# A tenth Strassen pair in three gate units, stage loads on SyncE, and other places for the Strassen steps

## Chip, cores and metric

One core of one Trainium2 chip. The metric is device microseconds of one execution; the program is run several times and the median is taken.

## What is computed

A decoder block over 256 tokens with 4096 channels, in fp32 (cut to the lines that cost time):

```python
h = rmsnorm(x, norm_w)                                       # 256 x 4096
u_p, z_p, u_c, b_c, c_c, z_c, g_logit = split(h @ w_in)      # w_in: 4096 x 20480
y_pool = causal_multiscale_pool(u_p, pool_w, pool_scale) * silu(z_p)
y_conv = causal_gated_shortconv(u_c, b_c, c_c, conv_w, conv_b) * silu(z_c)
br     = einsum('bsnc,ncd->bsnd', stack(y_pool, y_conv), w_branch)   # 2 x (2048 x 4096)
merged = sum_n sigmoid(g_logit + gate_b) * br
out    = rmsnorm(x + merged @ w_out, final_norm_w)           # w_out: 4096 x 4096
```

## The kernel before, in words

**Units and steps.** Every product is cut into units of 1024 output columns: 20 units on x (names cu, cc, cz, cb, pz, pu and the eight gate units g0_0 to g1_3, in the order g0_0, g1_0, g0_1, g1_1, g0_2, g1_2, g0_3, g1_3), 8 branch units (b0_0 to b1_3) and 4 output units (o0 to o3). A unit is a row of steps, 16 in the x and output units and 8 in the branch units. One step multiplies a pair of 128-channel blocks of the operand, kept in SBUF in `arena`, with 256 x 1024 weights that SyncE loads into one of three buffers `raw`. Two units carry the pooling as extra steps.

**Three products for one.** Each operand is held as a high part and the rest in fp32r, so that one product is three matmuls: high x high, high x rest, rest x high. For the weights ScalarE (ACT) writes the high part into `ring` and VectorE (DVE) the rest, by a subtraction (L72 is the one line that records all of DVE's tensor-tensor operations, L69 all of ACT's, L87, L91 and L94 the DMAs of SyncE and GpSimd; L1301 records the matmuls).

**P steps and Strassen steps.** A P step takes 2 token halves x 2 column halves x 2 blocks x 3 = 24 matmuls of 128x512. An S step does the 2x2 block product with 7 sums in place of 8 products (Winograd's form of Strassen): 21 matmuls. For it DVE must form weight sums: `V` (two sums, 128x1024), then `W` (two steps of 128x512), and split three of the raw blocks, V and W into `ring`. In a *helped* S step DMA forms V's sums: SyncE loads one block twice into a half of the tile E or R, GpSimd adds the other blocks to it with an accumulating DMA (`move_add`, L94), and `raw` gets 768 KB instead of 1024 KB. An S step needs the operand's own Strassen sums too, so only some pairs have them: x has 7 pairs stored plain (0 to 6) and 9 with sums (7 to 15).

**What sets the order.** The tables `PLACES` (and `OUT` for the output units) say at which of a unit's 16 steps the S steps stand; a unit with nine places uses the nine pairs 7 to 15 for them, and the others as P steps. `HELPED` says which S steps of a unit may be helped; whether one is depends on E or R being free by then. The preparation of weights runs up to three steps ahead of the matmuls, as far as `ring` (62 blocks; a P step takes 16, an S step 28) has room.

**Operands of the next stage.** From the end of g0_3 the places in `arena` that come free are filled with the operands of the branch units. `pop_fill`, called every 6 matmuls, starts a load of 256 KB from DRAM (`Fill.fetch`, by GpSimd's queue, L91) into one of the stages `sa`, `sb` or, during g1_3, the two halves of Y, and 8 calls later puts the work on it in the program: for a Strassen pair four sums on DVE, then a split on ACT and on DVE. In the output units the operands come from `m_d` in the same way.

**Gate units.** After the last Strassen product of a gate unit DVE joins the shared sums into R, GpSimd adds the bias by `move_add` (R<-in_gate_b, 1 MB), 12 calls later DVE adds E to R, ACT takes the sigmoid and GpSimd stores R to `gates_d`.

Of the kernel before, what the change touches and what calls it, by code (L numbers as in the profile page):

```python
# [26 lines left out]
F32 = mybir.dt.float32  # L27
F32R = mybir.dt.float32r
# [4 lines left out]
P = 128  # L33
T = 256
# [8 lines left out]
NP_X, NS_X = 7, 9  # L43
# [13 lines left out]
def hybrid_block(ctx: ExitStack, tc: tile.TileContext, x, x_t, norm_t, w_first, w_in, pool_w, pool_scale,  # L57
# [10 lines left out]
    def act(dst, src, func=AF.Copy, **kw):  # L68
        return pin(nc.scalar.activation(dst, src, func, **kw))  # L69
# [16 lines left out]
    def load(dst, src):  # L86
        return pin(nc.sync.dma_start(dst, src))  # L87

    def move(dst, src):

        return pin(nc.gpsimd.dma_start(dst, src))  # L91
# [8 lines left out]
    dram = ctx.enter_context(tc.tile_pool(name="dram", bufs=1, space=bass.MemoryType.DRAM))  # L100
# [33 lines left out]
    lower, upper = {}, {}  # L134
# [54 lines left out]
    Q3, Q5, Q6, Q7, A12, A22, A11, A21 = range(8)  # L189

    class Operand:


        def __init__(self, kind, view, region):
            self.kind, self.view, self.region = kind, view, region
            self.ready = False

        def block(self, part, i):

            return self.view[:, part, i]  # L200
# [373 lines left out]
    x_ops = make_ops(NP_X, NS_X, [("p", i) for i in range(NP_X)], [("s", i) for i in range(NS_X)])  # L574
# [43 lines left out]
    def at_places(at):  # L618
# [3 lines left out]

    few = NS_X - NB
    LAST_FIRST = ('cc0',)
    HELPED = {'cc0': (1, 2, 4, 5), 'cz0': (1, 2, 5), 'cb0': (1, 2, 4, 5, 7, 8), 'cu1': (1, 2, 4, 5, 7, 8), 'cc1': (1, 2, 4, 7, 8), 'cz1': (1, 2, 4, 5, 7), 'cb1': (1, 2, 4, 5), 'pz0': (1, 4, 5, 7), 'pu0': (1, 2, 4, 5, 7), 'pz1': (1, 4, 5, 6, 8), 'pu1': (1, 2, 4, 5, 7), 'g0_0': (1, 2, 4, 5, 7), 'g1_3': (1, 2, 5), 'g1_0': (1, 2, 4, 5, 8), 'g0_1': (1, 2, 4, 5, 6, 7), 'g1_1': (1, 4, 5, 7, 8), 'g0_2': (1, 2, 3, 4, 5, 7, 8), 'g1_2': (1, 2, 4, 5, 7, 8), 'g0_3': (1, 2, 4, 5, 7, 8), 'o0': (1, 2, 4, 5, 6), 'o1': (1, 2, 4, 5, 7), 'o2': (0, 1, 2, 4, 5), 'o3': (0, 2, 4, 5)}
    PLACES = {
# [308 lines left out]
    class Fill:  # L935
# [95 lines left out]
    for c in range(2):  # L1031
        i = units.index(with_band[c])
# [160 lines left out]
    queue = deque()  # L1193
# [160 lines left out]
    def run_step(u, st):  # L1354
        if st.kind == "B":
            band_sums(st)
            state["mm"] += 10
            after_group(u, ("F", 0, 0))
            return
        if st.kind == "M":  # L1360
            mix(st)
            state["mm"] += 24
            after_group(u, ("F", 0, 0))
            return
        for f in st.first:
            f()
        while not st.op.ready:
            pop_fill(True)
        assert st.kind != "S" or st.op.kind == "S"
        gs = st.groups()  # L1370
        for i, g in enumerate(gs):
            multiply(u, st, g)
            if i == len(gs) - 1:
                st.op.left -= 1

            if st is not steps[0] or i >= len(gs) // 2 - 1:
                after_group(u, g[0])
            if st is steps[0] and i == len(gs) // 2 - 1:
                warm_up(WARM_2)

    for u in units:
# [48 lines left out]
        pump()  # L1430
# [167 lines left out]
```

## Time and profile before

| what | value |
|---|---|
| median of 3 runs | 2368.99 us (2368.52 to 2370.82) |
| the profiled execution's own time | 2368.59 us |
| its span, first to last instruction | 2366.9 us |
| mean granted TensorE clock | 0.998 |
| PE busy (matmuls) | 2349.3 us, 99% of the span |
| DVE busy | 2192.1 us, 93% |
| ACT busy | 1423.9 us, 60% |
| POOL busy | 138.3 us, 6% |
| DMA moved | 596.44 MB, mean 252 GB/s |

The page gives busy time by engine and by groups of instructions. Where an engine was idle, the timeline shows the idle time in brackets before the instruction, with what ended it. A row of the timeline reads: start in us from the span's start, length in us, engine, line, operation, out<-in, shape, count. The windows view gives busy time and count of each engine in a stretch. POOL in the views is GpSimd, SP is SyncE, SPq and POOLq their DMA queues.

### The profile page before, as it was taken

To read this page: it belongs to the slowest core of one execution; us is meant where nothing else is said; L and a number is where in the kernel's file an instruction comes from. 1 tells how busy PE (TensorE), PEld (TensorE's weight loads), DVE (VectorE), ACT (ScalarE), POOL (GpSimd) and SP (SyncE) were. 2 spreads that over 40 slices of the span, in tenths; PEclk is the share of its full clock that TensorE was granted. 3 is DMA by queue.
4 is the path that set the end of the run, shared out by engine and by line. 5 is a ranking of instruction groups with operands and counts; after the bars stand their busy time and mean duration, and the time that the engine had idled before them with its cause. 6 is when DMAs were issued, how large, how long until landed. Compare 5 with 4: busy or idle time off the path is not lost.

```text
span 2366.9 us, 28142 instructions
## 1 busy us (share of the span) xinstructions
PE 2349.3 (99%) x10465; PEld 1943.7 (82%) x10465; DVE 2192.1 (93%) x2259; ACT 1423.9 (60%) x1481; POOL 138.3 (6%) x207
## 2 busy tenths in 40 slices
PE   9999999999999999999999999999999999999998
PEld 7888888888888888888888888888878888888886
DVE  8999999999999989989999999989899899899998
ACT  7565665656556656656666656565665566566555
POOL 0000000000001001000000000001100001000000
PEclk9999999999999999999999999999999999999999
DMA  8566678877777668656887898887866668778877
GB/s 337 179 235 212 242 273 255 262 238 232 258 260 244 226 226 253 232 211 229 273 284 246 276 284 258 257 307 243 273 230 233 243 241 282 250 229 286 264 244 274
DMA packets 107754, 596.44 MB, mean 252 GB/s; under 512 B 11424, under 2 KB 11680, under 8 KB 53984
## 3 DMA queue, kind: packets, MB, share of 16 engines
q1 hardware_dynamic: 84848, 499.98, 58.2%
q0 software_dynamic: 22336, 93.60, 16.7%
q8 instruction: 82, 1.34, 0.2%
q10 hardware_dynamic: 432, 1.07, 0.1%
q14 instruction: 56, 0.46, 0.1%
HBM read 562.09 MB, written 25.17 MB: 248 GB/s over the span
## 4 chain that ended last, share of the span: by engine, by line
PE 96%; DVE 2%; DMA 1%; ACT 1%; issue 0%; SPq 0%; DVEq 0%; ACTq 0%
PE sums L1301 70%; PE shared L1301 24%; PE shared L809 1%; DVE ring L72 1%; PE shared L528 1%; DMA raw<-in_w_in_dram 0%; ACT ring L69 0%; DVE R L72 0%; DMA raw<-in_w_out_dram 0%; DVE W L72 0%; PE shared L788 0%; SPq L87 0%; DVE V L72 0%; DVE arena L72 0%; PE shared L789 0%
## 5 line engine op out<-in xcount | busy, mean ns | idle before, releaser
L1301 PE MATMUL sums<-ring,arena 128*128 128x512 f32 x7551 | 1788.6, 390 | 4.7 <-DVE ring L72 2.5
L1301 PEld LDWEIGHTS sums<-ring,arena 128*128 128x128 f32 x7551 | 1414.2, 188 | 299.8 <-DVE ring L72 3.7
L72 DVE TENSOR_TENSOR ring<-raw,ring 128x1024 fp32r<-128x1024 f32 (+3 forms) x689 | 937.7, 1388 | 81.0 <-ACT ring L69 79.4
L69 ACT ACTIVATE ring<-raw 128x1024 fp32r<-128x1024 f32 (+3 forms) x689 | 794.3, 1186 | 234.5 <-PE sums L1301 126.9
L1301 PE MATMUL shared<-ring,arena 128*128 128x512 f32 x2556 | 646.9, 390 | 1.1 <-DVE ring L72 1.0
L1301 PEld LDWEIGHTS shared<-ring,arena 128*128 128x128 f32 x2556 | 480.5, 188 | 102.2 <-DVE ring L72 2.4
L69 ACT ACTIVATE ring<-W 128x1024 fp32r<-128x1024 f32 x213 | 226.3, 1062 | 396.3 <-DVE W L72 325.8
L72 DVE TENSOR_TENSOR ring<-W,ring 128x1024 fp32r<-128x1024 f32 x213 | 261.1, 1226 | 20.6 <-ACT ring L69 8.9
L69 ACT ACTIVATE ring<-V 128x1024 fp32r<-128x1024 f32 x154 | 163.1, 1059 | 171.8 <-DVE V L72 138.9
L72 DVE TENSOR_TENSOR V<-raw 128x1024 f32<-128x1024 f32 x154 | 187.8, 1219 | 10.4 <-DMA raw<-in_w_in_dram 7.6
L72 DVE TENSOR_TENSOR ring<-V,ring 128x1024 fp32r<-128x1024 f32 x154 | 187.8, 1219 | 3.5 <-ACT ring L69 3.5
L72 DVE TENSOR_TENSOR W<-W,raw 128x512 f32<-128x512 f32 x213 | 146.2, 687 | 0.0
L72 DVE TENSOR_TENSOR W<-V,raw 128x512 f32<-128x512 f32 x154 | 106.4, 691 | 4.6
L72 DVE TENSOR_TENSOR R<-R,E 128x1024 f32<-128x1024 f32 (+1 forms) x49 | 77.4, 1592 | 8.9 <-DMA R<-in_gate_b_dram 5.3
L94 POOL DMA_DIRECT2D E<-in_w_in_dram x34 | 29.5, 869 | 593.9 <-DMA E<-in_w_in_dram 311.5
L72 DVE TENSOR_TENSOR R<-R,shared 128x512 f32<-128x512 f32 x87 | 59.6, 685 | 2.2 <-ACT R L69 0.3
L69 ACT ACTIVATE arena<-sa 128x512 fp32r<-128x512 f32 (+2 forms) x49 | 25.5, 554 | 57.3 <-DVE sa L72 57.2
L72 DVE TENSOR_TENSOR ring<-E,ring 128x1024 fp32r<-128x1024 f32 x45 | 55.2, 1226 | 1.5 <-ACT ring L69 1.5
L69 ACT ACTIVATE E<-sums,rin 128x512 f32<-128x512 f32 x76 | 49.2, 681 | 11.7 <-PE sums L1301 11.7
L69 ACT ACTIVATE ring<-E 128x1024 fp32r<-128x1024 f32 x45 | 47.1, 1046 | 6.1 <-PE shared L1301 2.8
L72 DVE TENSOR_TENSOR W<-E,raw 128x512 f32<-128x512 f32 x41 | 28.3, 691 | 4.7 <-DMA E<-in_w_in_dram 2.3
L72 DVE TENSOR_TENSOR ring<-R,ring 128x1024 fp32r<-128x1024 f32 (+1 forms) x20 | 26.7, 1336 | 4.0 <-ACT ring L69 4.0
(146 smaller groups left out, 629.8 us busy)
## 6 DMA issues: line engine op xcount, KB each, us to landing
raw<-in_w_in_dram SPq DMA_DIRECT2D x267, 1024.0 KB, 4.9
raw<-in_w_branch_dram SPq DMA_DIRECT2D x64, 1024.0 KB, 5.4
raw<-in_w_out_dram SPq DMA_DIRECT2D x56, 1024.0 KB, 5.8
raw<-in_w_in_dram SPq DMA_DIRECT2D x51, 768.0 KB, 6.4
E<-in_w_in_dram SPq DMA_DIRECT2D x34, 512.0 KB, 7.1
E<-in_w_in_dram POOLq DMA_DIRECT2D x34, 512.0 KB, 9.4
R<-in_w_in_dram SPq DMA_DIRECT2D x17, 512.0 KB, 7.6
R<-in_w_in_dram POOLq DMA_DIRECT2D x17, 512.0 KB, 8.7
```

What stands on the lines that cost most here:

```text
L69: return pin(nc.scalar.activation(dst, src, func, **kw))
L72: return pin(nc.vector.tensor_tensor(out=dst, in0=a, in1=b, op=op))
L94: return pin(nc.gpsimd.dma_start(dst, src, accum_op=ALU.add))
L528: pin(nc.tensor.transpose(shared(j)[:, i * T + t * P:i * T + (t + 1) * P], src[:, t, c:c + P], ident))
L809: pin(nc.tensor.matmul(o, a[:, k, ts], b[:, k], start=(k, i) == (0, 0), stop=(k, i) == (3, 2)))
L1301: pin(nc.tensor.matmul(ps, lhs, rhs, start=n == 0, stop=n == u.total[b] - 1))
```

## The change

It does five things.

1. **A tenth pair.** Pair 6 (`LATE`) gets Strassen sums as well: `late_sums` forms them on DVE during the preparation of step 23 (the eighth step of cc0, which is a P step now) in the tile `sa`, and two DMAs of GpSimd put them into DRAM (`late_d`, 320 KB). During g0_0 GpSimd loads them back into `sa`, and four steps later `late_parts` splits them (one ACT and one DVE instruction of 128x640) into a new tile `late` that stands where Y stood; Y is not used between g0_0's pooling and g1_3.
2. **Ten S steps** in the units g0_1, g0_2 and g1_2 (their lists in `PLACES` have ten entries now). The other gate units keep nine, g1_3 seven.
3. **Places moved** in `PLACES` for cc0, cb0, cu1, cc1, cb1, pz0, g0_1, g1_1, g0_2, g1_2, g0_3, g1_3 and in `OUT` for o2 and o3. In all there are 216 S steps after, 213 before.
4. **`HELPED`** is another table: 131 steps may be helped instead of 114. In the built program the helped S steps are 60 after and 59 before (in E 40 and 41, in R 20 and 18).
5. **Stage loads** (`Fill.fetch`) are issued by SyncE (`load`) instead of GpSimd (`move`): 31 DMAs of 256 KB.

```diff
     class Operand:
...
+            self.more = None
...
         def block(self, part, i):
-            return self.view[:, part, i]
+            if self.kind == "S":
+                return self.view[:, part, i]
+            if i in self.more:
+                return self.more[i][:, part]
+            return self.view[:, part, {A12: 0, A22: 0}[i], int(i == A22)]
...
+    LATE_AT, LATE_IN = 23, 8
...
-        "g0_1": (4, 5, 7, 8, 9, 10, 12, 13, 15),
-        "g1_1": (2, 4, 5, 7, 8, 10, 12, 13, 15),
-        "g0_2": (2, 4, 5, 7, 8, 10, 12, 13, 15),
-        "g1_2": (2, 4, 5, 7, 8, 11, 12, 13, 15),
-        "g0_3": (2, 4, 5, 6, 8, 10, 12, 13, 15),
-        "g1_3": (3, 6, 7, 9, 10, 11, 14),
+        "g0_1": (2, 4, 5, 6, 8, 9, 10, 12, 13, 15),
+        "g1_1": (4, 5, 6, 7, 8, 10, 12, 13, 15),
+        "g0_2": (2, 4, 5, 6, 8, 9, 10, 12, 13, 15),
+        "g1_2": (2, 4, 5, 6, 8, 9, 10, 12, 13, 15),
+        "g0_3": (2, 4, 5, 8, 9, 10, 12, 13, 15),
+        "g1_3": (3, 4, 6, 9, 11, 13, 14),
...
         def fetch(self, st):
             self.at, self.st = now[0], st
-            move(flat(st), self.src)
+            load(flat(st), self.src)
...
+    LATE = NP_X - 1
+    def late_sums():
+        o = x_ops[LATE]
+        h, l = (o.view[:, part].bitcast(F32) for part in range(2))
+        q = sa[:, 4:8].rearrange("p (k t) c -> p k t c", t=2)
+        add(q, h, l)
+        q = q.rearrange("p k t c -> p k (t c)")
+        mul(q, q, rbc[:, None].to_broadcast([P, 2, T]))
+        sums_s(sa, [sa[:, i] for i in range(4, 8)])
+        mul(sa[:, Q3], sa[:, Q3], std)
+        move(late_d[:, 0:4], sa[:, 0:4])
+        move(late_d[:, 4], sa[:, A11])
...
+        def high():
+            q.append(replace_by("late", lower).tile([P, 2, 5, P], F32R, name="late"))
+            act(q[0][:, 0], sa[:, 0:5])
+        def low():
+            sub(q[0][:, 1], sa[:, 0:5], q[0][:, 0].bitcast(F32))
+            o.more = {b: q[0][:, :, i] for i, b in enumerate((Q3, Q5, Q6, Q7, A11))}
...
+    before(LATE_AT, late_sums)
...
+            if u.name == "g0_0" and st is u.steps[LATE_IN]:
+                move(sa[:, 0:5], late_d)
+            if u.name == "g0_0" and st is u.steps[LATE_IN + 4]:
+                queue.extend(late_parts())
```

**The queues around g1_3.** GpSimd's row before, from the helped sums of g0_3 to those of g1_3 (E and R hold the sums, sa, sb and Y are stages, y_d is the operand in DRAM):

```order
L94 DMA E<-in_w_in_dram 128x1024
L94 DMA R<-in_w_in_dram 128x1024
L91 DMA sa<-y_d 128x512
L94 DMA R<-in_gate_b_dram 128x2x1024
L91 DMA sa<-y_d 128x512
L91 DMA sb<-y_d 128x512
L94 DMA E<-in_w_in_dram 128x1024
L91 DMA sa<-y_d 128x512
L91 DMA gates_d<-R 128x2048
L91 DMA Y<-y_d 128x512
L91 DMA sb<-y_d 128x512
```

The same place on GpSimd after, and then what stands on SyncE there:

```order
L94 DMA R<-in_gate_b_dram 128x2x1024
L94 DMA E<-in_w_in_dram 128x1024
L91 DMA gates_d<-R 128x2048
L94 DMA E<-in_w_in_dram 128x1024
L94 DMA R<-in_w_in_dram 128x1024
L94 DMA R<-in_gate_b_dram 128x2x1024
L91 DMA gates_d<-R 128x2048
L91 DMA Y<-gates_d 128x2048
```

```order
L87 DMA E<-in_w_in_dram 128x2x512
L87 DMA sb<-y_d 128x512
L87 DMA raw<-in_w_in_dram 128x2048 x2
L87 DMA E<-in_w_in_dram 128x2x512
L87 DMA sa<-y_d 128x512
L87 DMA Y<-y_d 128x512
L87 DMA raw<-in_w_in_dram 128x2048
L87 DMA sb<-y_d 128x512
L87 DMA raw<-in_w_in_dram 128x1536
```

The stage loads have left GpSimd's row, where they stood behind accumulating DMAs, and stand between the weight loads of SyncE.

**DVE in a unit that gets the tenth pair.** Steps 6 and 7 of g0_2 (counted from 0), a P step and a helped S step before:

```order
L72 TENSOR_TENSOR ring<-raw,ring 128x1024 x2
L72 TENSOR_TENSOR W<-E,raw 128x512
L72 TENSOR_TENSOR ring<-raw,ring 128x3x512
L72 TENSOR_TENSOR W<-W,raw 128x512
L72 TENSOR_TENSOR ring<-E,ring 128x2x512
L72 TENSOR_TENSOR ring<-W,ring 128x2x512
```

and after, an S step that is not helped and a P step:

```order
L72 TENSOR_TENSOR V<-raw 128x1024
L72 TENSOR_TENSOR W<-V,raw 128x512
L72 TENSOR_TENSOR ring<-raw,ring 128x3x512
L72 TENSOR_TENSOR W<-W,raw 128x512
L72 TENSOR_TENSOR ring<-V,ring 128x2x512
L72 TENSOR_TENSOR ring<-W,ring 128x2x512
L72 TENSOR_TENSOR ring<-raw,ring 128x1024 x2
```

The steps of g0_2 are, with P, V (an S step that is not helped), E and R (helped, with the tile that holds the sums): `PPVPVVPEEPVPVEPR` before, `PPVPVVVPEVVPVEPE` after.

**DVE in g1_3.** Step 9 and the beginning of step 10 before:

```order
L72 TENSOR_TENSOR V<-raw 128x1024
L72 TENSOR_TENSOR sa<-sa 128x128 x4
L72 TENSOR_TENSOR W<-V,raw 128x512
L72 TENSOR_TENSOR ring<-raw,ring 128x3x512
L72 TENSOR_TENSOR W<-W,raw 128x512
L72 TENSOR_TENSOR arena<-sa,arena 128x512
L72 TENSOR_TENSOR arena<-sa,arena 128x384
L72 TENSOR_TENSOR ring<-V,ring 128x2x512
```

and after:

```order
L72 TENSOR_TENSOR V<-raw 128x1024
L72 TENSOR_TENSOR W<-V,raw 128x512
L72 TENSOR_TENSOR ring<-raw,ring 128x3x512
L72 TENSOR_TENSOR W<-W,raw 128x512
L72 TENSOR_TENSOR ring<-V,ring 128x2x512
L72 TENSOR_TENSOR sa<-sa 128x128 x4
L72 TENSOR_TENSOR ring<-W,ring 128x2x512
L72 TENSOR_TENSOR arena<-sa,arena 128x512
L72 TENSOR_TENSOR arena<-sa,arena 128x384
```

The four sums on the stage stand behind the split of V now. g1_3 is `PPPVPPVVPVVEPPVP` before and `PPPVVPVPPVPEPERP` after.

More of the change, by code (lines that the diff above doesn't have):

```diff
@@ L128, in hybrid_block @@
     m_d = dram.tile([4, P, 4, 2, T], F32, name="m_d")
+    late_d = dram.tile([P, 5, P], F32, name="late_d")
     z_d = dram.tile([2, P, 2, NU], F32, name="z_d")
@@ L624, in hybrid_block @@
     LAST_FIRST = ('cc0',)
-    HELPED = {'cc0': (1, 2, 4, 5), 'cz0': (1, 2, 5), 'cb0': (1, 2, 4, 5, 7, 8), 'cu1': (1, 2, 4, 5, 7, 8), 'cc1': (1, 2, 4, 7, 8), 'cz1': (1, 2, 4, 5, 7), 'cb1': (1, 2, 4, 5), 'pz0': (1, 4, 5, 7), 'pu0': (1, 2, 4, 5, 7), 'pz1': (1, 4, 5, 6, 8), 'pu1': (1, 2, 4, 5, 7), 'g0_0': (1, 2, 4, 5, 7), 'g1_3': (1, 2, 5), 'g1_0': (1, 2, 4, 5, 8), 'g0_1': (1, 2, 4, 5, 6, 7), 'g1_1': (1, 4, 5, 7, 8), 'g0_2': (1, 2, 3, 4, 5, 7, 8), 'g1_2': (1, 2, 4, 5, 7, 8), 'g0_3': (1, 2, 4, 5, 7, 8), 'o0': (1, 2, 4, 5, 6), 'o1': (1, 2, 4, 5, 7), 'o2': (0, 1, 2, 4, 5), 'o3': (0, 2, 4, 5)}
+    HELPED = {'cc0': (0, 1, 2, 4, 5), 'cz0': (1, 2, 5, 7), 'cb0': (1, 2, 4, 5, 7, 8), 'cu1': (1, 2, 4, 7, 8), 'cc1': (1, 2, 4, 7, 8), 'cz1': (1, 2, 4, 5, 7), 'cb1': (1, 2, 3, 4, 5), 'pz0': (1, 4, 5, 6, 7), 'pu0': (1, 2, 4, 5, 7), 'pz1': (4, 5, 6, 8), 'pu1': (1, 2, 4, 5, 7), 'g0_0': (1, 2, 4, 5, 7, 8), 'g1_3': (1, 2, 4, 5, 6), 'g1_0': (0, 1, 2, 4, 5, 6, 8), 'g0_1': (0, 1, 2, 3, 5, 8, 9), 'g1_1': (0, 1, 2, 3, 4, 5, 6, 7, 8), 'g0_2': (0, 1, 2, 3, 4, 8, 9), 'g1_2': (0, 1, 2, 3, 6, 7, 8, 9), 'g0_3': (0, 1, 2, 3, 4, 5, 6, 7, 8), 'o0': (1, 2, 3, 4, 5, 6), 'o1': (1, 2, 4, 5, 7), 'o2': (0, 1, 2, 4), 'o3': (0, 2, 4, 5)}
+    LATE_AT, LATE_IN = 23, 8
     PLACES = {
[1 row of a table removed]
[1 row of a table added]
         "cz0": (5, 7, 8, 9, 10, 12, 14, 15),
[3 rows of a table removed]
[3 rows of a table added]
         "cz1": (5, 6, 7, 9, 10, 11, 12, 14, 15),
[2 rows of a table removed]
[2 rows of a table added]
         "pu0": (3, 5, 7, 8, 10, 11, 13, 14),
@@ L858, in hybrid_block @@
     merged = {}
-    OUT = ((6, 7, 9, 11, 12, 13, 15), (2, 4, 5, 7, 8, 10, 11, 15), (2, 3, 4, 6, 10, 11, 13, 15), (1, 3, 4, 7, 9, 10, 12))
+    OUT = ((6, 7, 9, 11, 12, 13, 15), (2, 4, 5, 7, 8, 10, 11, 15), (2, 3, 4, 6, 10, 11, 12, 13), (1, 3, 5, 7, 9, 10, 12))
     def out_unit(c):
@@ L1154, in x_parts, with late_parts @@
             sub(o.view[:, 1, a:b], sa[:, a:b], o.view[:, 0, a:b].bitcast(F32))
+    LATE = NP_X - 1
[10 more added lines that the diff above has]
+        move(late_d[:, 4], sa[:, A11])
+    def late_parts():
+        o, q = x_ops[LATE], []
+        def high():
[4 more added lines that the diff above has]
+            o.more = {b: q[0][:, :, i] for i, b in enumerate((Q3, Q5, Q6, Q7, A11))}
+        return [high, low]
     def before(i, fn, *args):
@@ L1368, in run_step @@
             pop_fill(True)
-        assert st.kind != "S" or st.op.kind == "S"
+        assert st.kind != "S" or st.op.kind == "S" or st.op.more
         gs = st.groups()
```

12 rows, old and new, of the table PLACES are left out of this document.

## Prediction

> **What bounds the kernel now.** I read the page first, for the engine that is never idle.
>
> ```profile
> span 2366.9 us, 28142 instructions
> PE 2349.3 (99%) x10465; PEld 1943.7 (82%) x10465; DVE 2192.1 (93%) x2259; ACT 1423.9 (60%) x1481; POOL 138.3 (6%) x207
> L1301 PE MATMUL sums<-ring,arena 128*128 128x512 f32 x7551 | 1788.6, 390 | 4.7 <-DVE ring L72 2.5
> L1301 PE MATMUL shared<-ring,arena 128*128 128x512 f32 x2556 | 646.9, 390 | 1.1 <-DVE ring L72 1.0
> ```
>
> The matmuls set the time, and DVE with its 93% is close behind. The mean of 390 ns overlaps with the next matmul; the true step comes from an undisturbed piece of the chain of waits:
>
> ```profile
> 1983.10 66.64 PE sums L1301 x294
> ```
>
> 66.64 / 294 = 0.2267 us. So a P step takes 24 x 0.2267 = 5.44 us of PE, an S step 21 x 0.2267 = 4.76. Next, where PE does not run at that rate: the windows view of three stretches (PE is the second column, with its count), and one undisturbed for comparison.
>
> ```profile
> 1640.00:1665.00 25.00, 23.41 (x99) 18.01 (x98) 23.98 (x29) 15.21 (x16) 2.67 (x5) 1.00 0.49 166
> 1665.00:1685.00 20.00, 19.88 (x88) 16.14 (x87) 17.43 (x22) 14.77 (x19) 0.54 (x1) 1.00 0.85 301
> 1715.00:1735.00 20.00, 16.52 (x65) 12.92 (x64) 17.77 (x26) 13.51 (x18) 0.53 (x1) 0.91 0.76 299
> 1740.00:1765.00 25.00, 25.00 (x112) 20.70 (x111) 24.71 (x23) 13.71 (x14) 0.05 (x1) 1.00 0.58 203
> ```
>
> 112 matmuls in 25 us is the full rate, 89.6 in 20 us. Missing are 13, 1.6 and 24.6, times 0.2267: **2.95 + 0.36 + 5.58 = 8.89 us lost**, the first two in g1_3 and at the turn to b0_0, the third at the end of b0_0. The timeline shows the third from PE's side:
>
> ```profile
> 1721.22 0.50 PE L1301 MATMUL sums<-ring,arena 128*128 128x512 f32 x1 [1.46 <-ACT ring L69]
> 1723.74 0.83 PE L1301 MATMUL sums<-ring,arena 128*128 128x512 f32 x2 [2.02 <-DVE ring L72]
> 1724.38 4.44 PE L1301 MATMUL shared<-ring,arena 128*128 128x512 f32 x12
> ```
>
> After the two waits twelve matmuls take 4.3 us, not 2.7: the granted clock is down (0.91 over that window), so the waits cost more than their length. What DVE itself waited for before these places:
>
> ```profile
> 1631.36 1.22 DVE L72 TENSOR_TENSOR V<-raw 128x1024 f32<-128x1024 f32 x1
> 1636.29 1.02 DVE L72 TENSOR_TENSOR sa<-sa 128x128 f32<-128x128 f32 x4 [3.71 <-DMA sa<-y_d]
> 1703.89 1.23 DVE L72 TENSOR_TENSOR R<-R,E 128x1024 f32<-128x1024 f32 x1 [5.25 <-DMA R<-in_gate_b_dram]
> ```
>
> In g1_3 it stood 3.71 us for a stage, in b0_0 5.25 us for the gate bias. DVE works in order, so the splits of the weights stood too. GpSimd's queue says why the stage was late:
>
> ```profile
> 1624.50 0.90 POOL L94 DMA_DIRECT2D E<-in_w_in_dram  x1 [12.44 <-DMA E<-in_w_in_dram]
> 1625.07 0.89 POOL L91 DMA_DIRECT2D sa<-y_d  x1
> 1687.75 1.23 POOL L94 DMA_DIRECT2D R<-in_gate_b_dram  x1 [1.31 <-DVE R L72]
> ```
>
> The load of sa stood behind an accumulating DMA that waited 12.44 us for its own target to land. The bias add took 1703.89 - 1687.75 = 16.1 us.
>
> **The change part by part.** *Three more S steps.* Three P steps become S steps: 9 matmuls fewer, 9 x 0.2267 = **-2.04 us**, all on PE's path.
>
> *What DVE pays for them.* From start to start in the timeline:
>
> ```profile
> 1129.77 1.22 DVE L72 TENSOR_TENSOR V<-raw 128x1024 f32<-128x1024 f32 x1
> 1136.34 1.22 DVE L72 TENSOR_TENSOR V<-raw 128x1024 f32<-128x1024 f32 x1
> 1142.91 2.35 DVE L72 TENSOR_TENSOR ring<-raw,ring 128x1024 fp32r<-128x1024 f32 x2
> 1145.17 1.22 DVE L72 TENSOR_TENSOR V<-raw 128x1024 f32<-128x1024 f32 x1
> 135.84 0.69 DVE L72 TENSOR_TENSOR W<-E,raw 128x512 f32<-128x512 f32 x1
> 141.15 1.22 DVE L72 TENSOR_TENSOR ring<-raw,ring 128x1024 fp32r<-128x1024 f32 x1
> ```
>
> An S step costs DVE 6.57 us, a helped one 5.31, a P step 2.26. Against PE's 4.76 and 5.44 DVE's lead loses 1.81 in an S step, 0.55 in a helped one, and gains 3.18 in a P step. I call lead what lies between DVE's last split for a step and PE's first matmul of it. How low may it go? In g1_0:
>
> ```profile
> 1140.41 0.84 PE L1301 MATMUL shared<-ring,arena 128*128 128x512 f32 x3
> 1141.76 1.22 DVE L72 TENSOR_TENSOR ring<-W,ring 128x1024 fp32r<-128x1024 f32 x1
> ```
>
> PE began at 1140.41, DVE ended at 1142.98: a lead of -2.57 without a wait, for W is read by the last 6 of the 21 matmuls alone. The first split of a step ends 3.0 us before the last, so PE waits below about -3.0; in a unit's last S step, which reads W from the seventh matmul on, below -1.4.
>
> Now g0_2, whose first six steps stay. At step 4 the trace has:
>
> ```profile
> 1373.65 0.84 PE L1301 MATMUL shared<-ring,arena 128*128 128x512 f32 x3
> 1369.74 1.23 DVE L72 TENSOR_TENSOR ring<-W,ring 128x1024 fp32r<-128x1024 f32 x1
> ```
>
> Lead 1373.65 - 1370.97 = 2.7. Carried on with the new order VVPEVVPVE from step 5 (add PE's time of a step, take off DVE's of the next): 0.9, -0.9, 1.6, 1.7, -0.1, **-1.9**, 0.6, -0.5, -1.1. It never reaches -3.0, but at step 10 only 1.1 us is left. Data that come late fall on that rest. In the gate units before DVE did wait for data:
>
> ```profile
> 1389.44 0.69 DVE L72 TENSOR_TENSOR W<-E,raw 128x512 f32<-128x512 f32 x1 [2.31 <-DMA E<-in_w_in_dram]
> 1325.37 1.23 DVE L72 TENSOR_TENSOR V<-raw 128x1024 f32<-128x1024 f32 x1 [2.51 <-DMA raw<-in_w_in_dram]
> ```
>
> One such wait at the worst place costs 2.3 - 1.1 = 1.2 us of PE. Bounds for the three units: 0, if the waits fall elsewhere, and 3 x (2.51 - 1.1) = 4.2. I take one of three, **+1.2**.
>
> *The tenth pair's sums.* No row shows them; nearest are the same sums for another pair, from 164.93 to 167.71:
>
> ```profile
> 164.93 0.75 DVE L72 TENSOR_TENSOR sa<-arena 128x256 f32<-128x256 f32 x2
> 167.71 2.35 DVE L72 TENSOR_TENSOR ring<-raw,ring 128x1024 fp32r<-128x1024 f32 x2
> ```
>
> 2.8 us of DVE in cc0, and later one split of 640 columns (between 0.6 and 1.2 us, the 512 and 1024 column rows). Both fall into P steps, which give 3.2 of lead. On PE 0; without that cover at most 2.8 + 1.2 = 4.0. The three DMAs of 320 KB have some 10 us or more before anyone needs them; cost 0, upper bound the 3.7 us that a stage cost above. The other moved steps and the one additional helped step (1.26 us less of DVE) shift leads in units that never waited before: 0, within the 1.2 above.
>
> *Stage loads on SyncE.* SyncE does not wait for its loads, so the 12.44 us ahead of sa go. What lead g1_3 then has follows from its step 3, whose row up to there stays:
>
> ```profile
> 1611.65 0.84 PE L1301 MATMUL shared<-ring,arena 128*128 128x512 f32 x3
> 1607.21 1.22 DVE L72 TENSOR_TENSOR ring<-W,ring 128x1024 fp32r<-128x1024 f32 x1
> ```
>
> Lead 1611.65 - 1608.43 = 3.2. Carried with the order before (PPVVPVVEPPVP from step 4), each split of a fill taken at 0.6 and four sums at 0.9 us: 2.4 at step 9, 0 at 10, -2 at 11, -0.5 at 12; with the 3.71 us of the late stage step 11 stands at -5.7, beyond -3.0. With the order after (VPVPPVPEPE): 0.8, 3.3, 1.6, 3.5, 6, 4, 4.7, 3.1, 5.6, 5.1 from step 4 to 13. So DVE comes out ahead even if the stage were late by 3.71. **-3.31** (bounds -3.31 and 0). What may be late next is a weight load with a stage load ahead of it on SyncE:
>
> ```profile
> raw<-in_w_in_dram SPq DMA_DIRECT2D x267, 1024.0 KB, 4.9
> ```
>
> A quarter of that, for 256 KB, is 1.2 us, less than that lead.
>
> *b0_0.* The same bias add after has no stage loads beside it on GpSimd's queue, and DVE, not held up in g1_3, joins R earlier. The other such adds:
>
> ```profile
> R<-in_gate_b_dram POOLq DMA_DIRECT2D x7, 1024.0 KB, 12.5
> ```
>
> 12.5 in place of 16.1 us leaves a wait of 5.25 - 3.6 = 1.7 us for the same issue. How late b0_0's last step was:
>
> ```profile
> 1717.56 2.20 PE L1301 MATMUL sums<-ring,arena 128*128 128x512 f32 x9
> 1722.47 1.22 DVE L72 TENSOR_TENSOR ring<-W,ring 128x1024 fp32r<-128x1024 f32 x1
> ```
>
> The first three of the nine matmuls belong to the step before, so PE was due at 1717.56 + 3 x 0.2267 = 1718.24, and W's split ended at 1723.69: a lead of about -5.4. 3.6 better is -1.8, against the -1.4 that the last S step can bear: 0.4, taken as 0.5 us left of the 5.58, and the clock stays up. **-5.58 + 0.5** (bounds -5.58 and 0).
>
> **Sum** against the profiled execution's own 2368.59: -2.04 - 3.31 - 5.58 + 0.5 + 1.2 = -9.23, so 2359.36. The median of the runs shown is 0.40 above that execution: **2359.8 us**.
>
> **The rivals.**
>
> *Stage loads no earlier.* While sa was under way the DMA engines were full:
>
> ```profile
> 1630.00:1635.00 5.00, 5.00 (x24) 4.13 (x23) 2.58 (x3) 1.49 (x1) 0.00 (x0) 1.00 1.01 324
> ```
>
> A share of 1.01 says that what holds a load may be the transfer, not the queue, and on SyncE's own queue weight loads are ahead of it. Then both waits stay and only the matmuls go: 2368.99 - 2.04 = 2366.95. [...] Chance 0.12.
>
> *The bias stays late.* g1_3 recovers, the add still takes 16 us: 5.58 stays, 2359.8 + 5.08 = 2364.9. For it: DVE's join stands at the same place of its row, and DMA is full there. Chance 0.14.
>
> *The ten-pair units run dry.* The late data hit all three: 4.2 in place of 1.2, 2362.8. Chance 0.07.
>
> *Slower: SyncE stands before stage loads as GpSimd did.*
>
> ```profile
> POOL sa L91 <- DVE arena L72: 103.3, 9, 39.5
> ```
>
> GpSimd waited 103.3 / 9 = 11.5 us for a stage to come free. On SyncE every weight load queues behind that, then ACT's and DVE's splits, then PE. From about 8.5 us on (5.5 of lead and 3.0) PE pays the rest, 3.0 us for each of the six sa loads of that stretch: 2366.95 + 18 = 2385. Against it: the stage's last reader stands ahead, in DVE's own order, of the reader for which the next weight load waits anyway, so SyncE should find it free. Chance 0.07.
>
> **How the numbers follow.** The forecast has 0.60. Its own range is 2357.5 (nothing new is lost, 0.5 for the spread of runs) to 2363. The range takes in all but the slower rival: 2357.2 to 2367.2. 0.2% is 4.7 us, about what a measurement can tell from no change: faster is below 2364.3. That gives 0.60 + 0.07 and a third of the late bias for faster, 0.72; 0.21 for the same; 0.07 slower.
>
> **What would show it.** In the profile after: 10098 matmuls at L1301; in g1_3 no PE wait and no DVE wait for sa over 1 us; a bias add in b0_0 of about 12 us and no stretch of lower clock near 1720; PE waits of at most a few us in g0_1, g0_2, g1_2. I am wrong if DVE waits for raw there by more than 3 us at a time, or if SyncE's queue shows waits ahead of stage loads.

## The result and the profile after

The changed kernel takes 2359.65 us (median of 5 runs, 2359.49 to 2360.37), the kernel before 2368.99 us (5 runs, 2368.52 to 2370.88): a ratio of 0.9958, 95% interval 0.9946 to 0.9971. The forecast was 2359.8. The profiled execution took 2359.62 us, its span is 2357.9 us. Of all runs told of here one, of the experiment e8 (2901.57 us at a granted clock of 0.763), was in a slower state; it is left out of the intervals, and without it e8's median is 2365.08 in place of 2365.35. The page, and the groups of matmuls by shape:

```profile
span 2357.9 us, 28175 instructions
PE 2344.5 (99%) x10456; PEld 1941.8 (82%) x10456; DVE 2204.8 (94%) x2278; ACT 1426.4 (60%) x1485; POOL 125.0 (5%) x180
L1336 PE MATMUL sums<-ring,arena 128*128 128x512 f32 x7497 | 1776.1, 390 | 0.7 <-ACT ring L69 0.7
L1336 PE MATMUL shared<-ring,arena 128*128 128x512 f32 x2556 | 645.0, 389 | 0.0
L1336 PE MATMUL shared<-ring,late 128*128 128x512 f32 x36 | 9.4, 395 | 0.0
L1336 PE MATMUL sums<-ring,late 128*128 128x512 f32 x9 | 2.6, 396 | 0.0
```

7497 + 2556 + 36 + 9 = 10098 matmuls, 9 fewer than before. The idle time ahead of them was 4.7 and 1.1 us and is 0.7 and 0.0. The windows view of the three stretches where before lost time, and of the two ten-pair stretches where I feared new waits:

```profile
1640.00:1665.00 25.00, 25.00 (x112) 20.68 (x111) 24.31 (x29) 17.23 (x19) 0.86 (x1) 1.00 0.91 278
1665.00:1685.00 20.00, 20.00 (x90) 16.57 (x89) 18.32 (x24) 15.04 (x20) 1.22 (x1) 1.00 0.81 298
1715.00:1735.00 20.00, 20.00 (x89) 16.54 (x89) 19.86 (x23) 8.51 (x12) 0.00 (x0) 1.00 0.44 166
1185.00:1235.00 50.00, 50.00 (x222) 41.28 (x221) 49.34 (x48) 31.32 (x31) 3.53 (x4) 1.00 0.87 275
1350.00:1400.00 50.00, 50.00 (x221) 41.28 (x221) 49.26 (x48) 29.79 (x28) 3.54 (x4) 1.00 0.89 284
```

PE is busy all the time in each, at full clock; 222 matmuls in 50 us is the full rate. What is left of DVE's waits for data in g1_3 and b0_0:

```profile
1632.42 1.22 DVE L72 TENSOR_TENSOR V<-raw 128x1024 f32<-128x1024 f32 x1 [2.44 <-DMA raw<-in_w_in_dram]
1694.71 1.23 DVE L72 TENSOR_TENSOR R<-R,E 128x1024 f32<-128x1024 f32 x1 [1.41 <-DMA R<-in_gate_b_dram]
```

The wait of 3.71 us for sa is gone, the one for the bias went from 5.25 to 1.41 us, and a wait of 2.44 us for a weight load is new. The rows of SyncE (SPq) and GpSimd (POOL) ahead of it:

```profile
1622.59 0.33 SPq L87 DMA_DIRECT2D sa<-y_d  x1
1622.97 0.65 SPq L87 DMA_DIRECT2D Y<-y_d  x1
1627.74 0.33 SPq L87 DMA_DIRECT2D raw<-in_w_in_dram  x1
1628.16 0.98 SPq L87 DMA_DIRECT2D sb<-y_d  x1
```

```profile
1620.66 0.90 POOL L94 DMA_DIRECT2D E<-in_w_in_dram  x1 [13.75 <-DMA E<-in_w_in_dram]
1636.63 0.85 POOL L94 DMA_DIRECT2D E<-in_w_in_dram  x1 [11.93 <-DMA E<-in_w_in_dram]
1681.15 1.22 POOL L94 DMA_DIRECT2D R<-in_gate_b_dram  x1 [30.90 <-DVE R L72]
```

GpSimd still stands 12 to 14 us before these two accumulating DMAs. No stage load stands behind them any more.

The stage sa itself came no sooner. A load into sa can start when DVE has read the stage's old content. Before, that was the end of this row:

```profile
1621.95 0.68 DVE L72 TENSOR_TENSOR arena<-sa,arena 128x512 fp32r<-128x512 f32 x1
```

So sa was free at 1622.63. GpSimd's 12.44 us ended at 1624.50, so only the last 1.9 of them held this load up; issued at 1625.07 it was 2.4 us late, then took 11.2 us and landed at 1636.26. In the changed kernel sa was free at 1622.52, SyncE issued its load at 1622.59, and the load took 14.0 us and landed at 1636.59. DVE no longer waits because the four sums on the stage now stand behind the split of V and start later:

```profile
1637.69 1.01 DVE L72 TENSOR_TENSOR sa<-sa 128x128 f32<-128x128 f32 x4
```

DVE had lost 2.44 us to the weight load just before; without that loss it would, by these rows, have waited 1.3 us here.

### The profile page after: what moved, and what is told of

Its sections match the earlier page's. It is cut to its first block, busy times and chain, and to the rows that moved or that the text cites. A ratio compares the mean times of both kernels' runs of the same rounds, so it can differ in the third digit from the quotient of the medians.

```text
span 2357.9 us, 28175 instructions
## 1 busy us (share of the span) xinstructions
PE 2344.5 (99%) x10456; PEld 1941.8 (82%) x10456; DVE 2204.8 (94%) x2278; ACT 1426.4 (60%) x1485; POOL 125.0 (5%) x180
## 4 chain that ended last, share of the span: by engine, by line
PE 99%; DMA 0%; DVE 0%; ACT 0%; SPq 0%; DVEq 0%; issue 0%
PE sums L1336 72%; PE shared L1336 25%; PE shared L816 1%; PE shared L534 1%; DMA raw<-in_w_first_dram 0%; PE shared L795 0%; PE shared L796 0%; PE shared L798 0%; ACT V L69 0%; PE shared L797 0%; PE sums L1573 0%; DVE R L72 0%; DVE E L84 0%; DVE raw L1555 0%; ACT ring L69 0%; DVEq L1633 0%
## 5 line engine op out<-in xcount | busy, mean ns | idle before, releaser
L72 DVE TENSOR_TENSOR arena<-sa,arena 128x512 fp32r<-128x512 f32 (+2 forms) x50 | 28.5, 598 | 1.4 <-ACT arena L69 1.4
```

The lines of the kernel that those rows point to most:

```text
L72: return pin(nc.vector.tensor_tensor(out=dst, in0=a, in1=b, op=op))
```

## The experiments

From each trace I summed what PE lost: wherever two matmuls start more than 0.32 us apart, the excess over 0.2267 us (a lower clock is in it). Before lost 3.07 us in g1_3 and 5.57 us in b0_0 by this count (smaller gaps, 0.25 us in all, are not in it), the changed kernel nothing from 360 us on. The time from the last matmul to the end of the span varies with the same instructions, so the end of the last matmul is given too (us; the losses and the end are those of the profiled execution, which for e12 took 2377.36 us, 3.3 above the median, for the others within 1 us of it; medians of the runs, with the ratio's interval to the kernel before on the same chip, whose medians there were 2369.7, 2369.7 and 2369.0):

| kernel | median | ratio, interval | 1100-1510 (to g1_2) | to 1600 (g0_3) | to 1690 (g1_3, turn to b0_0) | to 1735 (b0_0) | later | last matmul ends |
|---|---|---|---|---|---|---|---|---|
| before | 2368.99 | | 0 | 0 | 3.07 | 5.57 | 0 | 2356.24 |
| changed | 2359.65 | 0.9946-0.9971 | 0 | 0 | 0 | 0 | 0 | 2346.28 |
| e1 | 2362.9 | 0.9960-0.9982 | 0 | 0 | 0 | 4.46 | 0 | 2350.49 |
| e2 | 2361.45 | 0.9954-0.9979 | 0.94 | 0.11 | 0 | 0 | 0.22 | 2348.73 |
| e3 | 2360.99 | 0.9952-0.9977 | 0 | 0 | 0 | 0.11 | 0.26 | 2347.85 |
| e4 | 2365.31 | 0.9975-0.9992 | 0 | 0 | 0 | 4.43 | 0 | 2352.22 |
| e5 | 2359.86 | 0.9952-0.9977 | 0 | 0 | 0 | 1.20 | 0.22 | 2348.00 |
| e6 | 2360.68 | 0.9957-0.9980 | 0.11 | 0 | 0 | 1.12 | 0.25 | 2347.76 |
| e7 | 2364.32 | 0.9975-0.9993 | 4.64 | 0 | 0 | 0.63 | 0.24 | 2351.64 |
| e8 | 2365.35 | 0.9975-0.9993 | 0.90 | 0 | 1.99 | 0.27 | 3.09 | 2352.32 |
| e9 | 2366.42 | 0.9981-0.9999 | 0 | 0 | 0.40 | 5.23 | 0 | 2352.81 |
| e10 | 2375.23 | 1.0016-1.0036 | 2.37 | 0.83 | 5.86 | 2.60 | 4.46 | 2362.28 |
| e11 | 2364.95 | 0.9976-0.9994 | 5.62 | 0 | 0 | 0 | 0 | 2352.29 |
| e12 | 2374.08 | 1.0011-1.0030 | 9.21 | 2.06 | 1.93 | 2.15 | 3.09 | 2365.04 |

My theory (A) was that GpSimd's queue held the stages back and that g1_3's new places would have covered a late stage besides; the rivals, that the loads' issuer did it alone (B), or the places alone (C).

**e1: the changed kernel, stage loads back on GpSimd.**

```diff
-            load(flat(st), self.src)
+            move(flat(st), self.src)
```

> The changed kernel with the 31 stage loads given back to GpSimd; everything else stays. Theory A (the queue held the stages, and g1_3's new places would cover a late stage): DVE waits 2 to 4 us for sa in g1_3 again, PE does not wait there; the bias add of b0_0 lands later by about 2.5 us (16 in place of 13.6) and takes b0_0's last step from a lead of -0.6 to about -3, so PE pays 0 to 2 us: 2359.7 to 2361.7. Theory B (SyncE's loads alone brought the time): both stalls return, 8.4 us, 2368. Theory C (the new places alone brought it): 2359.7, with no PE wait and the bias add no later.

The instruction streams of DVE and ACT are the changed kernel's, row by row; only the issuer differs. PE lost nothing in g1_3, but 4.46 us in b0_0: 2362.9 us, between A and B. The stage that came late was sb, which GpSimd issued at 1635.91 (SyncE at 1628.16), behind the accumulating DMA; here ACT's, DVE's and PE's rows:

```profile
1635.26 0.87 POOL L94 DMA_DIRECT2D E<-in_w_in_dram  x1 [10.36 <-DMA E<-in_w_in_dram]
1635.91 0.79 POOL L91 DMA_DIRECT2D sb<-y_d  x1
1646.41 0.63 ACT L69 ACTIVATE arena<-sb 128x512 fp32r<-128x512 f32 x1 [2.77 <-DMA sb<-y_d]
1648.45 1.76 DVE L72 TENSOR_TENSOR ring<-raw,ring 128x1536 fp32r<-128x1536 f32 x1 [3.08 <-ACT ring L69]
1715.50 0.49 PE L1336 MATMUL sums<-ring,arena 128*128 128x512 f32 x1 [0.38 <-ACT ring L69]
1718.02 1.09 PE L1336 MATMUL sums<-ring,arena 128*128 128x512 f32 x2 [2.03 <-DVE ring L72]
1718.90 4.18 PE L1336 MATMUL shared<-ring,arena 128*128 128x512 f32 x12
```

DVE stands 3.08 us for ACT, and ACT for the stage: the same fault by another way, since both kept the order of their rows. In g1_3 the lead goes down to -2.6, half a microsecond from the limit of -3.2 that e7 finds; the places cover it. In b0_0 they don't.

**e2: the kernel before, stage loads on SyncE.** Part 5 of the change alone.

```diff
-            move(flat(st), self.src)
+            load(flat(st), self.src)
```

> The kernel before with only the 31 stage loads moved to SyncE. Theory A: DVE no longer waits for sa in g1_3, the lead of the old places goes to about -2 at step 11, PE waits under 1 us there, and the bias add in b0_0 is no longer late: 2360.5 to 2361.5. Theory B: the same, 2360.5. Theory C (places alone): the stalls stay, 2367 to 2369.

2361.45 us: nothing lost in g1_3 and b0_0, the old places notwithstanding. So the issuer alone recovers both stalls; C falls. With the old places sa does come sooner: it is free at 1623.67, SyncE issues its load within 0.1 us, the load takes 7.9 us in place of 11.2, and DVE finds it there:

```profile
1633.65 1.02 DVE L72 TENSOR_TENSOR sa<-sa 128x128 f32<-128x128 f32 x4
```

So 2.4 us of the gain are the issue and 3.3 the transfer, with DMA engines no less full (a share of 1.05, 1.03 and 1.03 from 1620 to 1635, before 0.93, 0.96 and 1.01). (The 0.94 us in g1_2 is a wait of DVE for raw, 2.71 us, in a stretch where this program is that of before, which waited 2.02 there.)

**e4: the kernel before with g1_3's new places and HELPED entry alone.**

```diff
-        "g1_3": (3, 6, 7, 9, 10, 11, 14),
+        "g1_3": (3, 4, 6, 9, 11, 13, 14),
```

> The kernel before with only g1_3's seven places and its HELPED entry of the changed kernel; stage loads stay on GpSimd. Theory A: GpSimd still issues sa late and DVE still waits some 3 us, but with two more helped steps the lead stays above -3, g1_3 loses nothing; b0_0's bias add is joined earlier but lands late, PE pays 0 to 3 us there: 2360.5 to 2363.5. Theory B (loads alone): g1_3 and b0_0 lose as before, 2368 to 2369. Theory C (places alone): 2360.5 with both stalls gone.

2365.31 us: g1_3 loses nothing, though its lead goes down to -3.2, the limit itself; b0_0 loses 4.43. Each of the two parts covers g1_3 by itself, as A has it; b0_0 is recovered by the issuer only, and A was too mild there.

**e9: the kernel before, no helped step in g1_3.** This takes the accumulating DMA away from ahead of sa.

```diff
-'g1_3': (1, 2, 5)
+'g1_3': ()
```

> The kernel before, stage loads on GpSimd, but no step of g1_3 may be helped: one helped step (step 11) becomes a plain one, and the accumulating DMA that stood 12.44 us ahead of sa is gone. Theory A (that DMA held the stage): sa is issued some 12 us earlier, DVE waits less than 1 us for it; step 11 costs DVE 1.26 us more, the lowest lead is about -3.3 and PE loses under 1 us in g1_3; b0_0 begins with 2 us more of lead, loses 2 us in place of 5.6, and the clock stays up: 2361.5 to 2363.5. Rival (the full DMA engines held it): DVE still waits over 3 us for sa and the dearer step adds to it: 2369 to 2370.5.

2366.42 us. DVE doesn't wait for sa at all, and g1_3 and the turn to b0_0 lose 0.40 in place of 3.07. The load of sa is issued 0.4 us after the stage is free (2.4 before) and takes 4.2 us (11.2 before), with DMA engines nearly as full (a share of 0.95 and 0.98 from 1625 to 1635, before 0.96 and 1.01). So full engines alone did not hold the stage. The helped step's loads went with it, 0.75 MB, so this run doesn't part the accumulating DMA from its bytes. But b0_0 loses 5.23 as before, which neither theory had: in this kernel its stall is not handed on by DVE from g1_3, as my prediction said. What it is shows beside e2. GpSimd's stage loads at the turn to b0_0 in e9, and what ACT waited for:

```profile
1658.08 0.54 POOL L91 DMA_DIRECT2D sa<-y_d  x1 [19.96 <-ACT ring L69]
1658.61 0.54 POOL L91 DMA_DIRECT2D sb<-y_d  x1
1659.15 1.08 POOL L91 DMA_DIRECT2D Y<-y_d  x2
1669.99 2.01 ACT L69 ACTIVATE ring<-raw 128x1024 fp32r<-128x1024 f32 x2 [1.79 <-DMA raw<-in_w_branch_dram]
1685.69 2.01 ACT L69 ACTIVATE ring<-raw 128x1024 fp32r<-128x1024 f32 x2 [1.74 <-DMA raw<-in_w_branch_dram]
1700.46 1.23 DVE L72 TENSOR_TENSOR R<-R,E 128x1024 f32<-128x1024 f32 x1 [5.26 <-DMA R<-in_gate_b_dram]
```

The same in e2, SyncE and ACT:

```profile
1659.33 0.42 SPq L87 DMA_DIRECT2D sa<-y_d  x1
1661.23 9.17 SPq L87 DMA_DIRECT2D raw<-in_w_branch_dram  x3
1670.45 0.43 SPq L87 DMA_DIRECT2D sb<-y_d  x1
1692.61 1.06 ACT L69 ACTIVATE ring<-raw 128x1024 fp32r<-128x1024 f32 x1 [1.67 <-PE sums L1301]
1697.72 1.23 DVE L72 TENSOR_TENSOR R<-R,E 128x1024 f32<-128x1024 f32 x1 [2.19 <-DMA R<-in_gate_b_dram]
```

GpSimd, released late, sends four stages (1 MB) within 1.6 us, against the first weights of the branch units; ACT then waits for weights. On SyncE the four are spread over 12 us between the weights, and ACT waits for PE, that is, it is ahead.

**e5 and e6: half the loads each.** The change of issuer at step 12 of g1_3 (`units_done`): in e5 SyncE first, then GpSimd; in e6 the reverse.

```diff
-            load(flat(st), self.src)
+            (move if units_done[0] else load)(flat(st), self.src)
```

> The changed kernel with the stage loads on SyncE up to step 12 of g1_3 and on GpSimd from there on. Theory D (b0_0's stall is inherited: the late stages of g1_3 hold ACT and DVE, and b0_0 begins with 2.4 us less of lead): no late sb in g1_3, b0_0 begins with about 3.5 of lead as in the changed kernel, and PE pays 0 to 0.7 us at its end: 2359.7 to 2360.4. Rival E (the stage loads that stand beside the bias add on GpSimd's queue make it late): PE loses 2.8 us and the clock falls near 1716 as with all loads on GpSimd: 2362.9.

> The reverse: stage loads on GpSimd up to step 12 of g1_3, on SyncE from there on. Theory D: ACT waits 2.8 us for sb in g1_3 again, b0_0 begins with about 1 us of lead and PE loses some 2 to 4 us at its end, clock included: 2361.5 to 2363.5. Rival E: 2359.7, no PE wait near 1716.

2359.86 and 2360.68 us; b0_0 loses 1.20 and 1.12 us, so both halves count and neither theory has it alone (e5's time lies in D's range, its loss of 1.20 does not). The traces of nine kernels side by side (us; issue of the bias add after b0_0's first matmul, from issue to DVE's join, both together, lead of b0_0's last step, loss):

| kernel | issue | issue to join | sum | lead | PE lost |
|---|---|---|---|---|---|
| before | 7.3 | 16.1 | 23.5 | -5.5 | 5.57 |
| e9 | 7.3 | 15.8 | 23.0 | -5.1 | 5.23 |
| e1 | 6.8 | 15.1 | 22.0 | -4.4 | 4.46 |
| e4 | 7.3 | 14.6 | 22.0 | -4.3 | 4.43 |
| e10 | 6.8 | 14.9 | 21.6 | -4.0 | 2.60 |
| e5 | 5.0 | 15.2 | 20.2 | -2.6 | 1.20 |
| e6 | 6.7 | 13.5 | 20.1 | -2.5 | 1.12 |
| e2 | 5.0 | 14.0 | 19.0 | -1.4 | 0 |
| changed | 4.6 | 13.6 | 18.2 | -0.6 | 0 |

Stage loads on GpSimd up to step 12 of g1_3 delay the issue by some 2 us (e6 against the changed kernel, e1 against e5; the join of the shared sums stands in DVE's row behind splits that wait for late weights and stages); those behind it delay the landing by some 1.6 us. The lead follows the sum nearly one for one. Down to -1.4 it costs nothing; below, PE loses what is missing, 1.2 us at -2.6. Beyond -4 the lower clock adds some 1.6 us (8 matmuls of 0.427) in four of the five traces, not in e10. So two delays that cost 1.1 to 1.2 us each cost 4.46 together.

**e3: the changed kernel without the tenth pair.** The HELPED entries of the three units are those of before as well.

```diff
-        "g0_1": (2, 4, 5, 6, 8, 9, 10, 12, 13, 15),
+        "g0_1": (4, 5, 7, 8, 9, 10, 12, 13, 15),
...
-    before(LATE_AT, late_sums)
...
-                move(sa[:, 0:5], late_d)
...
-                queue.extend(late_parts())
```

> The changed kernel without the tenth pair: the lists and the HELPED entries of g0_1, g0_2 and g1_2 are those of before, and the sums of pair 6 are neither formed nor stored. If the tenth pair costs PE nothing, as the lack of PE waits in those units says, the time rises by the 9 matmuls, 2.04 us: 2361.7, with the unit turns 0.68 us later for each of the three units. Rival: late_sums in cc0 or the two stores at step 23 cost PE 0.2 us at 208.9 us and the start 0.3 us, which go too: 2361.2.

2360.99 us, and the last matmul ends 1.57 us later, not 2.04. 0.37 us are new small waits, and 0.46 us this execution was ahead at 341 us already; so the three steps are worth some 1.6 us (from g0_0's first matmul to g1_3's it takes 1.60 us longer). Why shows in the step lengths of the changed kernel's trace: an S step takes 4.76 us from first matmul to first matmul, a P step 5.44, but those of pair 6 take 4.88 and the step behind them 5.465. Their matmuls with an operand in `late` start 0.230 to 0.238 us apart, the others 0.227: 3 x 0.145 = 0.44 us of the 2.04 are lost there.

**e7: how low the lead may go.** Useless additions (which change nothing that is used) ahead of step 10.

```diff
+    for name, times in (("g0_1", 2), ("g0_2", 3), ("g1_2", 2)):
+        st = next(u for u in units if u.name == name).steps[10]
+        for _ in range(times):
+            before(steps.index(st), lambda: add(sa[:, 0:5], sa[:, 0:5], sa[:, 0:5]))
```

> The changed kernel with useless DVE additions of 128x640 (about 0.73 us each) ahead of step 10 of the ten-pair units: two in g0_1, three in g0_2, two in g1_2. The leads there are -2.8, -2.1 and -2.5 in the changed kernel. If PE waits only below about -3.0, the waits are 1.3, 1.3 and 1.0 us: 2363.2, with the clock up. Rival: the units have no reserve and each addition passes to PE in full, 5.1 us: 2364.8. Rival: something else carries PE there and the additions are hidden: 2359.7.

2364.32 us. PE's rows at the three places:

```profile
1242.86 0.72 PE L1340 MATMUL shared<-ring,arena 128*128 128x512 f32 x2 [1.08 <-DVE ring L72]
1405.70 0.74 PE L1340 MATMUL shared<-ring,arena 128*128 128x512 f32 x2 [1.22 <-DVE ring L72]
1487.94 0.73 PE L1340 MATMUL shared<-ring,arena 128*128 128x512 f32 x2 [1.52 <-DVE ring L72]
```

By the distance of the starts PE lost 1.24, 1.39 and 1.69 us there, at leads of -4.4, -4.6 and -4.9: the limit is at -3.2 each time. (The whole time, 2364.32, is nearer to the 2364.8 of "no reserve" than to my 2363.2; the single places decide: in g0_2 2.5 us less of lead cost 1.39.) I had expected 1.3, 1.3 and 1.0; g1_2 lost more because it began 0.9 lower than in the changed kernel, having got back less between the units. The changed kernel goes down to -2.8 in g0_1; its rows there:

```profile
1241.71 0.84 PE L1336 MATMUL shared<-ring,arena 128*128 128x512 f32 x3
1243.29 1.23 DVE L72 TENSOR_TENSOR ring<-W,ring 128x1024 fp32r<-128x1024 f32 x1
```

1241.71 - 1244.52 = -2.8: 0.4 us above the limit, and PE did not wait.

**e8, e11, e12: more ten-pair units.** In e8 g1_1 and g0_3 get the list of the three ten-pair units, and their tenth S step may be helped too:

```diff
-        "g1_1": (4, 5, 6, 7, 8, 10, 12, 13, 15),
+        "g1_1": (2, 4, 5, 6, 8, 9, 10, 12, 13, 15),
-        "g0_3": (2, 4, 5, 8, 9, 10, 12, 13, 15),
+        "g0_3": (2, 4, 5, 6, 8, 9, 10, 12, 13, 15),
```

In e11 g0_1, g1_1, g0_2 and g1_2 have ten, at other places, and every step of theirs may be helped (five are); in e12 g0_3 too:

```diff
-        "g1_2": (2, 4, 5, 6, 8, 9, 10, 12, 13, 15),
+        "g1_2": (2, 4, 5, 7, 8, 9, 11, 12, 13, 15),
```

> The changed kernel with ten S steps in g1_1 and g0_3 too, 218 S steps in all. Six matmuls fewer, 1.36 us. If the reserve holds there as in the other three units (lowest leads near -3): 2358.3; if each of the two runs into the limit by up to 1 us: 2359.3 to 2360.3.

> The changed kernel with ten S steps in g1_1 too, and in all four units at the places 2, 4, 5, 7, 8, 9, 11, 12, 13, 15, where five of the ten are helped in place of three; 217 S steps. Three matmuls fewer, 0.68 us, and 2 x 1.26 us more of lead in each unit. If the added helped sums come in time, no PE wait and 2359.0; if DMA can't bring them in time, waits of DVE of 2 to 4 us before some of them, and 2360 to 2363.

> The same places in g0_3 as well, 218 S steps in all: six matmuls fewer than the changed kernel. If the helped steps keep the lead at the turn to g1_3 above 4.5 us, g1_3 and b0_0 lose nothing: 2358.3. If g1_3 begins with less than that, as it did with unhelped places (3.7), its late stages show again: 2360 to 2365.

2365.35, 2364.95 and 2374.08 us: all worse than the changed kernel, and each above every value that I had given for it. In e8 g0_3 hands only 3.7 us of lead on to g1_3 (5.8 in the changed kernel), and g1_3 with the turn to b0_0 loses 1.99 us; most of the 3.09 us lost later fall in b1_0 and were not followed up. In e11 the added helped sums come late:

```profile
1302.80 0.69 DVE L72 TENSOR_TENSOR W<-E,raw 128x512 f32<-128x512 f32 x1 [0.90 <-DMA raw<-in_w_in_dram]
1311.01 0.69 DVE L72 TENSOR_TENSOR W<-E,raw 128x512 f32<-128x512 f32 x1 [2.00 <-DMA E<-in_w_in_dram]
```

The DMA share is 0.96 from 1200 to 1250 us and 1.02 from 1450 to 1500 there, 0.90 and 0.91 in the changed kernel. None of these three layouts bears more than three units with ten pairs; whether another does is open.

**e10: the tenth pair alone.** The kernel before with parts 1 and 2 of the change and cc0's place; `OUT`, the other places and HELPED entries and the stage loads' issuer as before.

```diff
+    before(LATE_AT, late_sums)
...
-        "g0_2": (2, 4, 5, 7, 8, 10, 12, 13, 15),
+        "g0_2": (2, 4, 5, 6, 8, 9, 10, 12, 13, 15),
```

> The tenth pair alone: the kernel before with pair 6's sums, cc0's place, and the ten places and HELPED entries of g0_1, g0_2 and g1_2; g0_3, g1_3 and all other places and GpSimd's stage loads as before. If the parts add up, the 9 matmuls come off and both stalls stay: 2366.95. Rival: the three units hand a lower lead on to g0_3 and g1_3, and the stalls there grow by up to 2 us: 2367 to 2369.

2375.23 us, slower than before by 0.16 to 0.36%, where I had 2366.95. The nine matmuls are gone, but PE loses at every place that has no reserve: 1.01 us at the end of g0_0 (the split into `late`), 1.36 in g0_2 and g1_2, 0.83 in g0_3, 5.86 in g1_3, 2.60 in b0_0, and 4.46 in the output units, whose tables are those of before: there a few splits change places in DVE's row, and in o2 DVE waits 5.47 us for weights where before waited 0.6; why was not followed up. Which of the moved places (part 3 of the change) repairs which of these was not tried one by one.

## Why the prediction was right, point by point

The profiled execution against its forecast (us). From g1_3's first matmul to b1_0's before took 133.3 us (1595.3 to 1728.7), the changed kernel 124.4 (1594.2 to 1718.7), with as many matmuls:

| term | forecast | measured |
|---|---|---|
| nine matmuls | -2.04 | -2.04 + 0.44 |
| g1_3 and b0_0 | -3.31 - 5.58 + 0.5 | -8.88 |
| new waits in ten-pair units | +1.2 | 0 |
| late sums, at 209 us | 0 | +0.19 |
| other, ahead of g0_0 | 0 | +0.33 |
| behind the last matmul | 0 | +0.98 |
| outside the span | 0 | +0.01 |
| sum | -9.23 | -8.97 |

- **Nine matmuls:** 10098 counted, as forecast. **The term was too large by 0.44**: I took the steps of pair 6 at the length of the others.
- **What DVE pays:** the carried leads were right within 0.2 to 0.4 us: at step 10 of g0_2 -1.9 forecast, -2.1 measured. **The +1.2 was wrong:** DVE waited for no data in g0_1, g0_2 and g1_2, and the one wait of 2.50 us left in the gate units before g1_3 stands in g1_1, where before had one of 2.51. e1 and e10, with the same ten-pair units, have no such wait there either, and e3, with nine pairs, has three; why the data are in time was not tried. The rival in which these units run dry falls with it.
- **Stage loads on SyncE:** the size is right, the reason half wrong. I took the whole 12.44 us as sa's delay; sa was free only 1.9 us before their end, and in the changed kernel it lands no sooner than before (1636.59 against 1636.26). g1_3 is saved there by the order, as my carried leads had it ("even if the stage were late by 3.71"), and e4 shows that the places alone do it. The queue did hold sb, by 7.75 us in e1, and e2 shows that with the old places the issuer alone recovers the loss. The leads carried for g1_3 were too high: 6, 4, 4.7, 3.1 forecast for steps 8 to 11, 5.7, 1.3, 1.4, -0.2 measured, for the weight load behind two stage loads came 2.44 us late, and I had priced that at 1.2. There was enough left.
- **b0_0:** the size is right, the reason half wrong. I put it down to a landing of 12.5 us in place of 16.1, with the same moment of issue; the landing took 13.6, and the other half is the issue, 2.7 us sooner after the unit's start. With the old places the stage wait in g1_3 was not what made it late (e9, 7.3 us without that wait); in e9 it is weights late behind the burst of stages. With the new places sb, late in g1_3, does it (e6, 6.7 us). The remaining 0.5 us was not paid.
- **Other moves at 0:** right for the changed kernel as a whole, wrong as a statement on what they do. By e10 the tenth pair doesn't stand without them and the issuer.
- **What is left** I take for scatter: cu1, the fifth unit, begins between 340.4 and 341.7 us in the fourteen traces (340.7 and 341.2 in these two), and from the last matmul to the end of the span pass 10.2 to 11.7 us (10.6 and 11.6), with the same instructions. That the forecast is off by only 0.15 us is chance: 1.7 us of waits that didn't come stand against 0.44 of slower matmuls and 1.5 at the beginning and the end, and the median lay 0.03 us above the profiled execution, not 0.40.
- **The rivals:** "stage loads no earlier" was so for sa in the changed kernel, but the waits did not stay; as a statement on the issuer it falls with e2. In the changed kernel the transfer gained nothing: a load of sa from y_d took 6.3 us from issue to landing on SyncE, 5.2 on GpSimd in the kernel before (medians of 11 and 10). What the issuer changed there was the moment of issue: sb's was 1628.16 in place of 1635.91 in e1. "The bias stays late" is e1, 2362.9 us where I had 2364.9. The slower rival didn't come, though its sign did: SyncE's queue stood before stage loads, 20.9 us in 13 waits of at most 4.9 us. I had called that a sign of being wrong; it cost PE nothing, and the longest wait of DVE for a weight load behind stage loads was the 2.44 us in g1_3.

## What to carry to other kernels

On GpSimd's queue a plain load stood behind a DMA that waited for another DMA, and it paid for that wait only from the moment its own buffer was free (1.9 of 12.44 us): look for the end of the buffer's last reader before the whole wait is priced. Here it paid to put such loads on the queue whose other loads they have to keep step with (3.07 and 5.57 us lost before, nothing there in e2). A wait can also vanish though its data come no sooner (sa landed at 1636.26 before and at 1636.59 after), because the instruction that waits has moved: look at the landing, too. Two parts of a change can each cover the same stall (the 3.07 us of g1_3, in e2 and in e4): measure each alone before the credit is given, and measure what they cost alone, too (here the tenth pair by itself was a loss, 2375.23 us in e10). Delays that added up in the lead did not add up in time: down to a lead of -1.4 they cost nothing (e2), and two of 1.20 and 1.12 us (e5, e6) cost 4.46 together (e1), some 1.6 of it by a lower clock.

## What the runs showed of the hardware

The matmuls with a stationary operand in the tile `late` start 0.230 to 0.238 us apart (0.234 in the mean), all others of that shape 0.227 in the mean; what about the tile does it wasn't tried.

The clock: in before, e1, e4 and e9 7 or 8 matmuls took 0.427 us each, 3.0 to 3.4 us in all, beginning at once to 1.3 us behind a wait of 2.29 us (with 0.4 to 1.6 us of another just ahead), and in e12 behind one of 1.99; in e10, after the same 2.29 us (0.2 just ahead), none did. The granted clock was 0.51 in before from 1724.2 to 1727.7 us, 0.91 in e12 from 1310 to 1330 and 1.00 in e10 from 1715 to 1735. So the length of the wait alone doesn't decide; what else does, no run here shows.

With four stage loads issued on GpSimd within 1.6 us weights came late (e9, ACT waits of 1.79 and 1.74 us); with the same four on SyncE, spread over 12 us between the weights, ACT waited for none at that place (e2). These two runs don't part the queue from the spacing.
